# Low parts on VectorE alone, keys split in place, and one factor a row in a single-core hybrid attention layer

## The chip, the cores and the metric

The kernel runs on one core of one Trainium2 chip. A core has five engines with a queue of instructions each: TensorE (PE; PEld are its weight loads), VectorE (DVE), ScalarE (ACT), GpSimd (POOL) and SyncE (SP), which here issues all DMAs. An engine takes its instructions strictly in the order in which they were written; engines wait for each other by semaphores. Matmul results land in PSUM (8 banks of 128x512 float32), everything else that engines work on lies in SBUF. The metric is the device time of one execution in microseconds (us); the kernel before takes 1096.38 us (median of 3 runs, 1095.64 to 1096.85).

## The reference

A decoder layer on x of 512x1024 in float32. All arithmetic is float32, and the output has to be that close to it.

```
h = rmsnorm(x, ln_mix_g);  proj = h @ w_in                 # 1024 x 7728
dq, dk, dv, nq, kc, vc, ksl, vsl, kwn, vwn, ng, mg = split(proj)
y_diff : 8 heads; a = softmax(q0 k0) - lam * softmax(q1 k1); rmsnorm(a @ dv) * subln_g * 0.2
y_nsa  : 16 heads in 4 groups; three attentions on one nq, each times its sigmoid gate:
         compressed blocks (a small MLP on kc, vc), selected blocks (ksl, vsl), window (kwn, vwn)
mixed = sigmoid(mg0) * (y_diff @ w_proj_diff) + sigmoid(mg1) * (y_nsa @ w_proj_nsa)
x = x + mixed @ w_out
x = x + square(relu(rmsnorm(x, ln_mlp_g) @ w_mlp_up)) @ w_mlp_down
```

With 512 tokens every block is selected and the window covers every earlier token, so the selected and the window branch are both plain causal attentions with their own keys and values (branch `b` = 0, 1). All queries and keys pass an rmsnorm per head and a rotation (rope).

## The kernel before

**Split numbers.** To keep float32 accuracy at the fast matmul rate, every factor of a matmul is split into two float32r tiles, a high part (a copy with rounding) and a low part (the factor minus its high part), by `split` (line 462): `copy` may be placed on ACT or DVE, the subtraction on the engines in `lo_engs`. A product is then three matmuls: high-high, high-low, low-high. A weight matrix streams through `WStream` (line 393) in pieces of 128x1024: a DMA into `wraw`, then for each half of 512 columns a high part `whi` and a low part `wlo`; two buffers of each, and a piece is prepared while the one before it is used. `add` in line 1541 registers the pieces of each GEMM and names DVE and POOL as the engines that may make the low parts.

**Streams.** The work is written as Python generators that `Pe.run` (line 72) interleaves by an estimate of TensorE's time: `rope_stream` (norm, rope, transposition and splitting of queries and keys), `side_stream` (compressed blocks), `value_stream` (probabilities transposed, split, and multiplied with values), `score_stream` (scores and softmax), and `filler` (all GEMMs in a fixed order: projections, merge gates, output projections, MLP). GEMM matmuls stand between those of the attention on TensorE's queue.

**Planner.** No instruction is issued where it is written: `Sched.note` (line 205) records it with its dependencies and, for each engine that may run it, a price (`price`, line 167); `flush` (line 272) is a list scheduler that takes the engine that is free first, picks the ready instruction that was written first, and so sets every engine's order and the choice of engine. It models one port that DVE and POOL share: `ported` (line 196) says which instructions hold it, and in lines 323 to 334 an engine whose first choice would find the port taken looks for a ready one that doesn't need it, and otherwise takes the first choice and lets it wait. The instructions themselves carry no trace of this port, it only moves their order.

**Keys.** `k_dups` (line 889) gets four transposed 128x128 blocks in a PSUM bank `ptp`: 64 partitions of one key, 64 of another. It splits the bank into the single buffer `kp`, and four DMAs copy each key's 64 partitions to both halves of its own tile `kk`, as the score matmul wants the key twice, once beside the high and once beside the low part of the query.

**Sparse probabilities.** In `score_stream` (line 1050) each tile of scores `sb` becomes `p` (mask and minimum on DVE, exponential with a row sum on ACT); then DVE makes the reciprocal of the row sum and multiplies `p` with two factors a row, the reciprocal and the gate (lines 1105 to 1107). There are two `p` buffers for each of the three larger widths and four for the smallest.

Names in the rows: `gb`, `ga` GEMM banks; `sb` scores; `sm`, `smn` row statistics of the differential and the sparse heads; `ptn`, `pta` transposed probabilities; `ah`, `al` their parts; `rw`, `t1r`, `t2r`, `str` the rope's; `hT` the normed input; `u`, `rr` the squared ReLU. All instructions are issued from line 357, so tiles tell them apart.

Of the kernel before, what the change touches and what calls it, by code (L numbers as in the profile page):

```python
# [12 lines left out]
F32R = mybir.dt.float32r  # L13
AF = mybir.ActivationFunctionType
# [117 lines left out]
class Sched:  # L132
# [34 lines left out]
    def price(self, eng, method, aps, k):  # L167
        if "accum_out" in k:
            aps = [x for x in aps if x is not k["accum_out"]]
        n = max(self.size(x) for x in aps)  # L170
        psum = any(self.tiles[x.tensor.name].space == "PSUM" for x in aps if x.tensor.name in self.tiles)
        if eng == "PE":
            if method == "transpose":
                return 113.0
            return max(113.0, 5.5 + self.size(aps[-1]) * 0.4315)
        if eng == "ACT":
            return (51 if psum else 93) + n * 0.8333 + (93 if "accum_out" in k else 0) + (
                93 if any(self.size(x) == 1 for x in aps[1:]) and n > 1 else 0)
        if eng == "DVE":
            ptr = sum(1 for x in aps[1:] if self.size(x) == 1) if n > 1 else 0  # L180
            if method in ("tensor_scalar", "tensor_copy") and not psum:
                return 69 + n * 0.52 + 61 * ptr
            if method == "memset":
                return 8 + n * 1.04
            if method == "reciprocal":
                return 69 + n * 6.25
            return 69 + n * 1.042 + 61 * ptr
        if eng == "POOL":
            if k.get("op") == OP.pow:
                return 300 + n * 165.0  # L190
            return 150 + n * 2.1
        return 20.0
# [2 lines left out]

    def ported(self, eng, method, aps, k):

        if max(self.size(x) for x in aps) < 64:
            return False
        if eng == "POOL":  # L200
            return k.get("op") != OP.pow
        return eng == "DVE" and method in self.TWICE and not any(
            self.tiles[x.tensor.name].space == "PSUM" for x in aps if x.tensor.name in self.tiles)

# [67 lines left out]
    def flush(self):  # L272

        ops, self.ops = self.ops, []
        self.wait = {e: [] for e in self.free}
        ok = {e: [] for e in self.free}
        fresh, again = [], set()
        for op in ops:
            for b in op.bufs:
                if b.group is None or b in again:  # L280
                    continue
                again.add(b)
                if b.granted:
                    self.held[b.group] += 1
                else:
                    fresh.append(b)
        for b in fresh:
            self.held.setdefault(b.group, 0)
            self.queue.setdefault(b.group, []).append(b)
        for op in ops:  # L290
            op.left, op.ready = 1, 0.0
            for d in op.deps:
                if d.left == -1:
                    op.ready = max(op.ready, d.end + self.lat(d.eng, op.eng, op.deps[d]))
                else:
                    d.users.append(op)
                    op.left += 1
            for b in op.bufs:
                if not b.granted:
                    b.waiting.append(op)  # L300
                    op.left += 1
        for g in list(self.queue):
            self.grant(g, 0.0)
        for op in ops:
            self.arm(op)
        done = []
        while len(done) < len(ops):
            best = None
            for e in self.free:
                for h, k in ((self.wait[e], 2), (ok[e], 1)):  # L310
                    while h and h[0][k].left == -1:
                        heapq.heappop(h)
                t = self.free[e] if ok[e] else max(self.free[e], self.wait[e][0][0]) if self.wait[e] else None
                if t is not None and (best is None or t < best[0]):
                    best = (t, e)
            assert best is not None, "no instruction can go on"
            t, e = best
            while self.wait[e] and self.wait[e][0][0] <= t:
                _, p, op = heapq.heappop(self.wait[e])
                if op.left == 0:  # L320
                    heapq.heappush(ok[e], (p, op))
            p, op = heapq.heappop(ok[e])
            if op.port[e] and self.port > t:
                put_off = [(p, op)]
                while ok[e] and put_off[-1][1].port[e]:
                    z = heapq.heappop(ok[e])
                    if z[1].left == 0:
                        put_off.append(z)
                if not put_off[-1][1].port[e]:
                    p, op = put_off.pop()  # L330
                else:
                    p, op = put_off.pop(0)
                for z in put_off:
                    heapq.heappush(ok[e], z)
            op.eng = e
            op.start = max(t, self.port) if op.port[e] else t
            op.end = op.start + op.ways[e][1]
            if op.port[e]:
                self.port = op.end
            self.free[e] = op.end  # L340
            if op.dma:
                self.hw = max(op.end, self.hw) + op.dma[0]
                self.dma = max(self.hw + 650, self.dma) + op.dma[1]
                op.end = self.dma
            op.left = -1
            done.append(op)
            for u in op.users:
                u.ready = max(u.ready, op.end + self.lat(e, u.eng, u.deps[op]))
                self.arm(u)
            for b in op.bufs:  # L350
                b.left -= 1
                b.end = max(b.end, op.end)
                if b.left == 0 and b.group is not None:
                    self.held[b.group] -= 1
                    self.grant(b.group, b.end + 150)
        for op in sorted(done, key=lambda o: o.start):
            op.ways[op.eng][0](*op.a, **op.k)  # L357
            op.ways = op.a = op.k = op.users = op.deps = None
# [68 lines left out]
def hybrid_block(ctx: ExitStack, tc: tile.TileContext, x, ln_mix_g, w_in, dqg, dkg, lq1, lk1, lq2, lk2,  # L427
# [22 lines left out]
    def f(ap):  # L450
        return ap.bitcast(F32)
# [3 lines left out]

    def copy(out, src, engs=("ACT", "DVE")):
        sched.note([(e, COPY[e], getattr(sched.engs[e], COPY[e])) for e in engs], (out, src), {})

    def tt(out, a, b, op, engs=("DVE",)):
        sched.note([(e, "tensor_tensor", sched.engs[e].tensor_tensor) for e in engs], (out, a, b), {"op": op})  # L460

    def split(hi, lo, src, hi_engs=("ACT", "DVE"), lo_engs=("DVE",)):

        copy(hi, src, hi_engs)
        tt(lo, src, f(hi), OP.subtract, lo_engs)
# [99 lines left out]
    with ExitStack() as ps:  # L565
# [322 lines left out]

        def k_dups(pt, key):

            kp = att.tile([128, 2, 512], F32R, tag="kp", bufs=1, name="kp")
            split(kp[:, 0, :], kp[:, 1, :], pt)
            if key[0] == "dk":
                kk = k_tile()
                dst = [kk[:, s] for s in range(2)]
            else:

                if key[2] == 0:
                    for s in range(2):
                        group_keys[key[1], s] = k_tile()  # L900
                dst = [group_keys[key[1], s][:, key[2]] for s in range(2)]
            for s in range(2):
                for d in range(2):
                    Q.dma_start(f(dst[s][d * 64:(d + 1) * 64]), f(kp[s * 64:(s + 1) * 64]))
            return dst

        jobs = []
# [142 lines left out]
        def score_stream():  # L1050
# [25 lines left out]
            for p in range(2):  # L1076
# [8 lines left out]
                for h in range(8):  # L1085
                    head = p * 8 + h
                    for b, i in [(b, i) for b in range(2) for i in reversed(range(NT))]:
# [14 lines left out]
                        for b_ in bs:  # L1102
                            st = att.tile([128, 12], F32, tag="sm", bufs=8, name="smn")
                            pr = softmax_num(sb[:, b_ * 128:] if i == 0 else sb, i, st[:, 0:2])
                            V.reciprocal(st[:, 3:4], st[:, 1:2])
                            V.tensor_scalar(pr[:, :n], pr[:, :n], st[:, 3:4],
                                            gates[:, i, head * 3 + 1 + b_:head * 3 + 2 + b_], op0=OP.mult, op1=OP.mult)
                            probs[head, b_, i] = pr
                            there(("pn", head, b_, i)).after(P_LAT + 2.5 * n)
                        s_use(S_LAT + n * len(bs))  # L1110
# [430 lines left out]
        def add(gen, pieces):  # L1541
            for piece in pieces:
                load, width = piece if isinstance(piece, tuple) else (piece, 1024)
                ws.add(load, ("DVE", "POOL"), width)
            plan.append(gen)

        def eight(src):
# [101 lines left out]
```

## Time and profile before

| | us |
|---|---|
| median of 3 runs | 1096.38 |
| the profiled execution | 1096.69 |
| its span, first to last instruction | 1094.9 |
| busy in it: PE, DVE, ACT, POOL | 1053.8, 766.2, 465.6, 477.0 |

The profile is of one execution. Busy time of PE is not work at full rate: its matmuls overlap in the record, and a matmul that waits behind another counts as busy. Whether TensorE runs at full rate is seen in how many matmuls start in a stretch. From about 765 us on the kernel is the MLP; up to about 654 us the attention runs beside the projections; what lies between are the output projections.

### The profile page before, as it was taken

The numbers are of one execution on the slowest core, as the hardware profiler recorded it, in microseconds if no ns is written. First come the engines' busy times: TensorE is split into PE (matmuls) and PEld (weight loads), VectorE is DVE, ScalarE is ACT, GpSimd is POOL, SyncE is SP. The second block draws the span as 40 slices with busy tenths as digits, with TensorE's granted clock in tenths as the row PEclk, the third lists the DMA queues.
The fourth block names the chain that finished last, engine by engine and source line by source line (L and its number), as shares of the span: only waits on it lengthen the run. The fifth ranks groups of instructions, "written<-read, shape, count | busy, mean of one in ns | idle before, by whom it ended". The sixth has DMA issues, their size and how long they took to land.

```text
span 1094.9 us, 15737 instructions
## 1 busy us (share of the span) xinstructions
PE 1053.8 (96%) x5257; PEld 875.6 (80%) x5257; DVE 766.2 (70%) x1905; ACT 465.6 (43%) x1136; POOL 477.0 (44%) x475
## 2 busy tenths in 40 slices
PE   6999988899999999999999998999999999999998
PEld 5877867788787888887788886788888888888886
DVE  6779678899988999999989898556533323354232
ACT  4257335656464466665456563214222111242110
POOL 3745698348767372292212024423333222333221
PEclk9999988999999999999999999999999999999999
DMA  6362534642654224536363255622322223332232
GB/s 209 97 173 63 153 102 120 163 132 71 172 143 142 64 78 137 142 125 214 129 193 112 92 161 170 208 85 94 96 97 97 97 96 96 97 97 96 97 136 75
DMA packets 83616, 134.66 MB, mean 123 GB/s; under 512 B 8784, under 2 KB 33872, under 8 KB 83536
## 3 DMA queue, kind: packets, MB, share of 16 engines
q1 hardware_dynamic: 83536, 133.67, 39.7%
q8 instruction: 41, 0.67, 0.3%
q14 instruction: 39, 0.32, 0.1%
HBM read 106.64 MB, written 14.42 MB: 111 GB/s over the span
## 4 chain that ended last, share of the span: by engine, by line
PE 74%; DVE 12%; DMA 6%; POOL 4%; issue 2%; SPq 1%; ACT 1%; DVEq 0%; POOLq 0%; ACTq 0%
PE gb L357 38%; PE ga L357 22%; PE sb L357 4%; PE avn L357 4%; PE ptn L357 3%; DMA kk<-kp 3%; DVE p L357 2%; POOL str L357 1%; PE av L357 1%; POOL wlo L357 1%; SPq L357 1%; POOL t1r L357 1%; DVE al L357 1%; DVE sm L357 1%; DMA kk<-in_x_dram 1%
## 5 line engine op out<-in xcount | busy, mean ns | idle before, releaser
L357 POOL TENSOR_TENSOR wlo<-wraw,whi 128x512 fp32r<-128x512 f32 x203 | 289.0, 1432 | 522.7 <-ACT whi L357 396.2
L357 ACT CAST whi<-wraw 128x512 fp32r<-128x512 f32 (+2 forms) x217 | 130.0, 618 | 343.7 <-PE gb L357 167.0
L357 DVE CAST whi<-wraw 128x512 fp32r<-128x512 f32 x97 | 47.5, 489 | 199.7 <-PE ga L357 95.8
L357 PE MATMUL gb<-wlo,hTh 128*128 128x512 f32 (+2 forms) x352 | 136.0, 388 | 4.4 <-POOL wlo L357 2.4
L357 PE MATMUL gb<-whi,hTl 128*128 128x512 f32 (+2 forms) x352 | 135.0, 384 | 0.0
L357 PE MATMUL gb<-whi,hTh 128*128 128x512 f32 (+2 forms) x352 | 133.4, 388 | 1.5 <-ACT hTh L357 1.3
L357 DVE CUSTOM_DVE_ANT_0 p<-sb,cst 128x512 f32<-128x512 f32 (+2 forms) x192 | 92.1, 481 | 13.1 <-PE sb L357 11.7
L357 DVE TENSOR_TENSOR wlo<-wraw,whi 128x512 fp32r<-128x512 f32 (+1 forms) x111 | 92.2, 832 | 7.2 <-ACT whi L357 2.7
L357 ACT ACTIVATE p<-p,smn 128x512 f32<-128x512 f32 (+3 forms) x128 | 72.0, 563 | 26.6 <-DVE smn L357 26.2
L357 PEld LDWEIGHTS gb<-wlo,hTh 128*128 128x128 f32 x352 | 67.7, 192 | 14.8 <-POOL wlo L357 3.4
L357 PEld LDWEIGHTS gb<-whi,hTh 128*128 128x128 f32 x352 | 66.7, 191 | 11.5 <-ACT hTh L357 1.7
L357 PEld LDWEIGHTS gb<-whi,hTl 128*128 128x128 f32 x352 | 67.6, 192 | 10.3 <-DVE hTl L357 0.3
L357 DVE TENSOR_SCALAR p<-p,smn,gates 128x512 f32<-128x512 f32 (+3 forms) x128 | 66.9, 527 | 1.0
L357 PE MATMUL gb<-big,whi 128*128 128x512 f32 x192 | 65.1, 403 | 0.0
L357 PE MATMUL gb<-hTl,whi 128*128 128x512 f32 x160 | 64.7, 404 | 0.0
L357 PE MATMUL gb<-hTh,wlo 128*128 128x512 f32 x160 | 64.5, 403 | 0.0
L357 PE MATMUL gb<-hTh,whi 128*128 128x512 f32 x160 | 64.0, 400 | 0.0
L357 DVE TENSOR_TENSOR al<-ptn,ah 128x128 fp32r<-128x128 f32 (+3 forms) x128 | 61.3, 482 | 3.6 <-ACT ah L357 2.0
L357 PE MATMUL ga<-h2l,whi 128*128 128x512 f32 x160 | 62.5, 391 | 0.0
L357 PE MATMUL ga<-h2h,whi 128*128 128x512 f32 x160 | 62.4, 391 | 0.0
L357 PE MATMUL ga<-h2h,wlo 128*128 128x512 f32 x160 | 62.3, 390 | 0.0
L357 ACT CAST ah<-ptn 128x384 fp32r<-128x384 f32 (+3 forms) x98 | 41.2, 424 | 49.1 <-PE ptn L357 38.1
(248 smaller groups left out, 2634.7 us busy)
## 6 DMA issues: line engine op xcount, KB each, us to landing
wraw<-in_w_in_dram SPq DMA_DIRECT2D x36, 512.0 KB, 3.6
wraw<-in_w_mlp_up_dram SPq DMA_DIRECT2D x32, 512.0 KB, 3.8
wraw<-in_w_mlp_down_dram SPq DMA_DIRECT2D x32, 512.0 KB, 3.5
kk<-kp SPq DMA_DIRECT2D x48, 256.0 KB, 4.5
wraw<-in_w_in_dram SPq DMA_DIRECT2D x36, 256.0 KB, 3.2
big<-yd SPq DMA_DIRECT2D x16, 512.0 KB, 3.4
yd<-yo SPq DMA_DIRECT2D x8, 512.0 KB, 3.3
wraw<-in_w_proj_diff_dram SPq DMA_DIRECT2D x8, 512.0 KB, 4.3
```

The costliest lines, as they stand in the source:

```text
L357: op.ways[op.eng][0](*op.a, **op.k)
```

## The change

Four edits, and one in the planner that goes with them. The low parts of weights may only be made by DVE (all but the first chunk, which is registered in another place and keeps both engines). `k_dups` has no `kp` any more: it splits each key's 64 partitions straight into its own half of `kk`, and one DMA a key copies that half to the other. A sparse tile is multiplied with one factor a row: the product of reciprocal and gate is made first, as 128x1 on DVE or POOL, and the product with `p` may go to DVE or ACT. In the planner, an engine whose ready choices all need the taken port now stays open until the port is free or something else becomes ready; DVE instructions of fewer than 64 elements a row count as holding the port too; and a 128x1 `scalar_tensor_tensor` costs one pointer more.

```diff
-            ptr = sum(1 for x in aps[1:] if self.size(x) == 1) if n > 1 else 0
+            ptr = sum(1 for x in aps[1:] if self.size(x) == 1) if n > 1 else method == "scalar_tensor_tensor"
...
     def ported(self, eng, method, aps, k):
-        if max(self.size(x) for x in aps) < 64:
-            return False
         if eng == "POOL":
-            return k.get("op") != OP.pow
+            return k.get("op") != OP.pow and max(self.size(x) for x in aps) >= 64
...
-                if not put_off[-1][1].port[e]:
+                go = not put_off[-1][1].port[e]
+                if go:
                     p, op = put_off.pop()
-                else:
-                    p, op = put_off.pop(0)
                 for z in put_off:
                     heapq.heappush(ok[e], z)
+                if not go:
+                    self.free[e] = min(self.port, self.wait[e][0][0]) if self.wait[e] else self.port
+                    continue
             op.eng = e
-            op.start = max(t, self.port) if op.port[e] else t
+            op.start = t
...
+    def scaled(out, src, factor):
+        sched.note([("DVE", "tensor_scalar", lambda o, x, c: nc.vector.tensor_scalar(o, x, c, None, op0=OP.mult)),
+                    ("ACT", "activation", lambda o, x, c: nc.scalar.activation(o, x, AF.Copy, scale=c))],
+                   (out, src, factor), {})
...
         def k_dups(pt, key):
-            kp = att.tile([128, 2, 512], F32R, tag="kp", bufs=1, name="kp")
-            split(kp[:, 0, :], kp[:, 1, :], pt)
...
             for s in range(2):
-                for d in range(2):
-                    Q.dma_start(f(dst[s][d * 64:(d + 1) * 64]), f(kp[s * 64:(s + 1) * 64]))
+                own, other = slice(s * 64, s * 64 + 64), slice(64 - s * 64, 128 - s * 64)
+                split(dst[s][own, 0], dst[s][own, 1], pt[own])
+                Q.dma_start(f(dst[s][other]), f(dst[s][own]))
...
                             V.reciprocal(st[:, 3:4], st[:, 1:2])
-                            V.tensor_scalar(pr[:, :n], pr[:, :n], st[:, 3:4],
-                                            gates[:, i, head * 3 + 1 + b_:head * 3 + 2 + b_], op0=OP.mult, op1=OP.mult)
+                            tt(st[:, 4:5], st[:, 3:4], gates[:, i, head * 3 + 1 + b_:head * 3 + 2 + b_], OP.mult,
+                               ("DVE", "POOL"))
+                            scaled(pr[:, :n], pr[:, :n], st[:, 4:5])
...
-                ws.add(load, ("DVE", "POOL"), width)
+                ws.add(load, ("DVE",), width)
```

Since the planner sets the order, the edits move instructions on every engine. By count over the whole program: low parts of weights on DVE 111 before and 313 now, on POOL 203 before and 1 now; products with sparse probabilities on DVE 128 before, now 45 there and 83 on ACT; the new 128x1 products 27 on DVE and 101 on POOL; high parts of weights on DVE 97 and 104, on ACT 217 and 210; high parts `ah` of transposed probabilities on DVE 40 and 53, on ACT 120 and 107; copies of projections `rw` out of PSUM on DVE 10 and 13; rope products and sums on DVE 75 and 97, on POOL 125 and 103; subtractions for keys on DVE 12 of 128 partitions before, 24 of 64 now; DMAs of keys 48 before, 24 now. TensorE has the same 5257 matmuls.

DVE, keys of the sixth differential head, before (`qa`, `qb` are the parts of the queries of the same job):

```order
L357 SCALAR_TENSOR_TENSOR p<-p,sm 128x512
L357 CAST kp<-ptp 128x512
L357 ISA p,sm<-sb,cst 128x384
L357 ISA sm 128x1
L357 TENSOR_TENSOR kp<-ptp,kp 128x512
L357 TENSOR_TENSOR qa<-ptp,qa 64x512
L357 TENSOR_TENSOR qb<-ptp,qb 64x512
```

and the same place now:

```order
L357 CAST kk<-ptp 64x512
L357 RECIPROCAL sm<-sm 128x4
L357 ISA p,sm<-sb,cst 128x384
L357 ISA sm 128x1
L357 TENSOR_TENSOR kk<-ptp,kk 64x512
L357 SCALAR_TENSOR_TENSOR sm<-sm,lam 128x1
L357 TENSOR_SCALAR ys<-yt,sm 128x128
L357 CAST kk<-ptp 64x512
L357 TENSOR_TENSOR qa<-ptp,qa 64x512
L357 TENSOR_TENSOR kk<-ptp,kk 64x512
L357 TENSOR_TENSOR qb<-ptp,qb 64x512
```

One split of 128 partitions into `kp` has become two of 64 into `kk`, with other work between them.

POOL, in the differential heads, before (`sm` are the row statistics of a finished head's output):

```order
L357 TENSOR_TENSOR t2r<-rw,ropes 128x4x32
L357 TENSOR_TENSOR t1r<-t1r,t2r 128x512
L357 TENSOR_TENSOR sm<-sm,epsc 128x1
L357 TENSOR_TENSOR sm<-sm,mhalf 128x1
L357 TENSOR_TENSOR wlo<-wraw,whi 128x512 x4
L357 TENSOR_TENSOR sm<-sm,epsc 128x1
L357 TENSOR_TENSOR sm<-sm,mhalf 128x1
L357 TENSOR_TENSOR wlo<-wraw,whi 128x512 x2
```

and now:

```order
L357 TENSOR_TENSOR str<-str,epsc 128x8
L357 TENSOR_TENSOR str<-str,mhalf 128x8
L357 TENSOR_TENSOR t2r<-rw,ropes 128x4x32 x2
L357 TENSOR_TENSOR t1r<-rw,ropec 128x256
L357 TENSOR_TENSOR sm<-sm,epsc 128x1
L357 TENSOR_TENSOR sm<-sm,mhalf 128x1
```

The low parts between the statistics and the rope's steps are gone from POOL's queue.

DVE, in the sparse heads, before:

```order
L357 RECIPROCAL smn<-smn 128x1
L357 ISA p,smn<-sb,cst 128x384
L357 ISA smn 128x1
L357 TENSOR_TENSOR pc<-sc,st_1557 128x256
L357 TENSOR_SCALAR p<-p,smn,gates 128x512
L357 ISA p,smn<-sb,cst 128x256
L357 ISA smn 128x1
L357 RECIPROCAL smn<-smn 128x1
L357 TENSOR_SCALAR p<-p,smn,gates 128x384
L357 CAST ah<-ptn 128x128
```

and now, a little later in the same stage:

```order
L357 RECIPROCAL smn<-smn 128x1
L357 TENSOR_TENSOR al<-ptn,ah 128x256
L357 CAST whi<-wraw 128x512
L461 TENSOR_SCALAR p<-p,smn 128x512
L357 TENSOR_TENSOR al<-ptn,ah 128x384
L357 RECIPROCAL smn<-smn 128x1
L357 ISA p,smn<-sb,cst 128x256
L357 ISA smn 128x1
L357 TENSOR_TENSOR wlo<-wraw,whi 128x512
L357 TENSOR_TENSOR al<-ptn,ah 128x512
L357 CAST ah<-ptn 128x128
L357 TENSOR_TENSOR wlo<-wraw,whi 128x512
```

One of the two products with `p` has left DVE's queue, and two low parts of weights stand in it.

## Rows read from the trace of the kernel before

**Rows 1.** Page, parts 1 and 2: busy time by engine, TensorE's clock by slice

```profile
PE 1053.8 (96%) x5257; PEld 875.6 (80%) x5257; DVE 766.2 (70%) x1905; ACT 465.6 (43%) x1136; POOL 477.0 (44%) x475
...
PEclk9999988999999999999999999999999999999999
```

**Rows 2.** Page, part 4: the chain that ended last, by engine, by line

```profile
PE 74%; DVE 12%; DMA 6%; POOL 4%; issue 2%; SPq 1%; ACT 1%; DVEq 0%; POOLq 0%; ACTq 0%
PE gb L357 38%; PE ga L357 22%; PE sb L357 4%; PE avn L357 4%; PE ptn L357 3%; DMA kk<-kp 3%; DVE p L357 2%; POOL str L357 1%; PE av L357 1%; POOL wlo L357 1%; SPq L357 1%; POOL t1r L357 1%; DVE al L357 1%; DVE sm L357 1%; DMA kk<-in_x_dram 1%
```

**Rows 3.** The chain from 765 us: start, length, what, count

```profile
873.43 43.52 PE ga L357 x192
```

**Rows 4.** Stretches: width; PE, PEld, DVE, ACT, POOL busy (instructions); PEclk, DMA share, GB/s

```profile
0.00:150.00 150.00, 138.47 (x687) 114.59 (x688) 113.58 (x271) 71.34 (x168) 86.75 (x97) 1.00 0.44 130
150.00:210.00 60.00, 50.13 (x249) 40.65 (x247) 49.20 (x120) 31.49 (x78) 39.30 (x46) 0.86 0.57 149
210.00:654.00 444.00, 432.91 (x2412) 364.64 (x2411) 411.82 (x1204) 262.43 (x713) 208.32 (x242) 1.00 0.43 131
...
765.00:1095.00 330.00, 326.02 (x1438) 269.57 (x1436) 119.04 (x197) 66.32 (x111) 103.01 (x67) 1.00 0.30 98
```

**Rows 5.** Timeline of PE: start, us, operation, [idle before it, and who ended it]

```profile
157.46 0.70 PE L357 MATMUL ptp<-cst,rw 128*128 128x128 f32 x4 [2.76 <-DVE kp L357]
...
175.65 0.80 PE L357 MATMUL gb<-wlo,hTh 128*128 128x512 f32 x1 [1.82 <-DVE wlo L357]
...
199.84 0.50 PE L357 MATMUL sb<-kk,qa 128*128 128x256 f32 x2 [2.40 <-DVE sm L357]
```

**Rows 6.** Timeline of DVE at three places

```profile
16.84 2.47 DVE L357 TENSOR_TENSOR hTl<-ga,hTh 128x512 fp32r<-128x512 f32 x4
...
173.77 1.22 DVE L357 SCALAR_TENSOR_TENSOR sm<-sm,lam 128x1 f32<-128x1 f32 x1
...
198.62 0.69 DVE L357 CAST kp<-ptp 128x512 fp32r<-128x512 f32 x1 [2.84 <-DMA kk<-kp]
```

**Rows 7.** Stretch of half clock, columns as in rows 4

```profile
175.00:180.00 5.00, 4.35 (x15) 3.75 (x16) 5.00 (x13) 1.29 (x3) 5.00 (x4) 0.50 0.36 105
```

**Rows 8.** Waits of PE, 0 to 660 us: total us, times, longest

```profile
PE sb L357 <- DVE sm L357: 7.5, 10, 2.4
...
PE gb L357 <- POOL wlo L357: 2.4, 2, 1.7
PE gb L357 <- DVE wlo L357: 2.0, 2, 1.8
```

**Rows 9.** Tile wlo in stretches: PE, PEld, DVE, POOL busy (instructions), then as rows 4

```profile
0.00:150.00 150.00, 69.32 (x188) 35.91 (x189) 20.74 (x22) 36.48 (x27) 1.00 0.44 130
150.00:210.00 60.00, 19.45 (x54) 11.25 (x54) 2.31 (x3) 15.73 (x12) 0.86 0.57 149
210.00:654.00 444.00, 159.06 (x416) 78.80 (x417) 18.13 (x21) 101.62 (x78) 1.00 0.43 131
```

**Rows 10.** Groups by form: busy us, mean ns of one, idle before

```profile
L357 DVE TENSOR_TENSOR wlo<-wraw,whi 128x512 fp32r<-128x512 f32 x110 | 91.7, 834 | 7.2 <-ACT whi L357 2.7 <-issue 0.4
L357 DVE TENSOR_TENSOR al<-ptn,ah 128x512 fp32r<-128x512 f32 x32 | 21.8, 681 | 1.3 <-ACT ah L357 0.6 <-PE ptn L357 0.6
L357 POOL TENSOR_TENSOR wlo<-wraw,whi 128x512 fp32r<-128x512 f32 x201 | 287.6, 1439 | 522.7 <-ACT whi L357 396.2 <-DVE whi L357 51.2 <-PE ga L357 19.3
L357 POOL TENSOR_TENSOR sm<-sm,epsc 128x1 f32<-128x1 f32 x32 | 11.8, 368 | 29.5 <-ACT ysq L357 29.5
```

**Rows 11.** Page, parts 5 and 6: groups, and DMA issues (KB each, us to landing)

```profile
L357 ACT ACTIVATE p<-p,smn 128x512 f32<-128x512 f32 (+3 forms) x128 | 72.0, 563 | 26.6 <-DVE smn L357 26.2
L357 DVE TENSOR_SCALAR p<-p,smn,gates 128x512 f32<-128x512 f32 (+3 forms) x128 | 66.9, 527 | 1.0
...
kk<-kp SPq DMA_DIRECT2D x48, 256.0 KB, 4.5
```

**Rows 12.** Tile kp: who ended the idle time before its instructions (us, times)

```profile
  DMA kk<-kp: 11.4, 6
```

## The prediction

> **What bounds the kernel now.** I read the page's busy times and TensorE's clock first, then the chain, then stretches, and last the single waits. The reader is to see that TensorE looks busy for 96% of the span [rows 1], but that only 74% of the chain is TensorE's; VectorE holds 12% of it, DMAs 6%, GpSimd 4% [rows 2]. The last third settles itself: there 192 matmuls of 512 columns take 43.52 us, 0.227 us each, and the chain is nothing but TensorE [rows 3], at a clock of 1.00 [rows 4]. From 765 us on there is nothing to gain. So the question is about 0 to 654 us, where the attention runs beside the projections. There VectorE is busy for 113.6 + 49.2 + 411.8 = 574.6 us, 88%, and in 210 to 654 us for 411.8 of 444, 92.8% [rows 4]; GpSimd is busy for 334.4 us. TensorE and VectorE feed each other through few buffers, and both are nearly full.
>
> The worst stretch is 150 to 210 us. TensorE's granted clock is 0.86 there on average [rows 4], and 0.50, its lower level of 1.2 GHz, in 175 to 180 us [rows 7]; at 0.86, 60 x 0.14 = 8.4 us of full-rate work are lost. What TensorE did before: it stood still for 2.76 us until VectorE had split keys, for 1.82 us until a low part of a weight came, and for 2.40 us until a row statistic freed a score bank [rows 5]. The first and the third go back to the buffer `kp`: in front of the third VectorE stands for 2.84 us at a key's copy, whose buffer a DMA is still reading [rows 6]. The second low part came late because the operation ahead of it, of one element a row, took 1.22 us, twice what a 128x512 operation costs [rows 6].
>
> **Low parts.** GpSimd makes 27 + 12 + 78 = 117 of them before 654 us [rows 9], and these go to VectorE. A recorded 128x512 operation takes 0.68 us on VectorE when one input is in PSUM; a row of four takes 2.47 [rows 6], so each further one costs (2.47 - 0.68) / 3 = 0.60, and the last 0.08 of a record overlaps with the next. 117 x 0.60 = +70.2 us of VectorE. On GpSimd they took 1.44 us each [rows 10], so a piece's low half is made in less than half the time once its turn comes.
>
> What comes back is the time in which the two engines hold each other up. A low part on VectorE, both inputs in SBUF, takes 0.834 us on average, the operation of the same shape with an input in PSUM 0.681 [rows 10]: 0.153 us, or 18%, is lost beside GpSimd. The share of GpSimd's busy time that goes away is 153.8 of 334.4, 46% [rows 4, 9]. If nothing comes back, 0; if all of VectorE's 574.6 us suffered like the low parts, 0.18 x 0.46 x 574.6 = 48. I take 30, nearer the upper end, since the low parts are the long ones of GpSimd's instructions. The Trainium skill ("SBUF — State Buffer", section "Who interferes with whom") says that a VectorE instruction with two SBUF inputs and a GpSimd instruction that reads SBUF shut each other out, whichever starts first, for the whole instruction. By that rule the trace agrees for the low parts (0.834 against 0.681), and each that is left on GpSimd could cost up to its own 1.44; worked out from it, as an estimate, the relief would lie above my 30.
>
> **Keys.** Twelve splits of 128 partitions become 24 of 64. The time goes by the 512 columns, so VectorE gets 12 more subtractions, +7.2 us; the extra copies go to ScalarE, which is busy for 262.4 of 444 us [rows 4]. Half of the 48 DMAs of 4.5 us each [rows 11] go, all in SP's queue, which only gets shorter. What goes from the path is the wait for `kp`: it ended 11.4 us of idle time [rows 12], of which TensorE saw 2.76 and 2.40 [rows 5]: -5.2. Late next is the key's own tile: the split now writes where the score matmuls of an earlier head read, but these stand earlier in TensorE's queue.
>
> **Sparse probabilities.** 83 of 128 products leave VectorE. One takes 0.527 recorded [rows 11], 0.447 without the overlap: -37.1 us. ScalarE gets 83 operations like the exponential, at most 0.563 each [rows 11], 46.7 us; it has 181 free in 210 to 654. 27 small products on VectorE cost 2 us at most. 101 go to GpSimd at 0.368, the row of its 128x1 addition [rows 10]: 37 us, less than the 101.6 that its low parts leave there. So a link is added: reciprocal, GpSimd, then ScalarE, behind whose product casts of weights and probabilities queue. If GpSimd is late, TensorE waits for these casts; the free time on GpSimd is the cover, and without it the price is bounded by 83 x 0.368 = 31 us of ScalarE, inside its 181. I take 0.
>
> **Planner.** The port rule and the load move a further 22 rope instructions, 13 high parts and 3 copies to VectorE, at most 0.60 each, 23 us; many are shorter, I take 15.
>
> **The sum.** VectorE up to 654 us: 574.6 + 70.2 + 7.2 + 15 + 2 - 37.1 - 30 = 601.9, 92% instead of 88%. What that costs I read in 210 to 654, where it is fullest: 411.8 + 78 x 0.60 + 3.6 (half of the keys) + 10 (of the 15) - 37.1 = 435.1, less two thirds of the relief, 20, is 415.1. If VectorE can again be kept busy for 92.8%, the stretch takes 447.3 us instead of 444: +3.3, I take +4 with the part before 210, where VectorE stays under 90%. Gains: keys -5.2; the two low-part waits of TensorE, 2.4 and 2.0 [rows 8], -4.4; the half clock of 150 to 210 us, -8.4, because the waits ahead of it go. Together -18 + 4 = -14. The MLP gives nothing and takes nothing: its 67 low parts on GpSimd [rows 4] cost VectorE 40 us on top of 119 of 330, and a piece lasts 24 x 0.227 = 5.4 us against 1.2 for its two low parts. If they got stuck behind the squared ReLU, a us at each of eight blocks would be 8 us. So the span goes from 1094.9 to 1080.9; the execution takes 1.8 us more than its span, and it was 0.3 above the median: 1082.5 us.
>
> **Rivals.** A, slower: VectorE becomes the bound in 210 to 654 us. For it speak the 92.8%, and that 70 us of work come onto the engine that most of TensorE's waits already name [rows 8]; against it, that ScalarE takes 37 off. Without any relief 435.1 / 0.928 = 468.9 us, +24.9, less 5.2 for the keys: 1116; with some, anything from 1098 up, 1107 in the middle. It decides where the relief in this stretch is under about 6 us, since (435.1 - 6) / 0.928 - 444 = 18 eats all gains. The Trainium skill's "Perfetto Trace Analysis", section "Optimizing Scalar/DVE Operations", speaks for A: where VectorE is saturated, it advises handing work to ScalarE or even GpSimd, the opposite of what is done with the low parts; it adds that between VectorE and GpSimd this might not help, because of their common port. Which half of it holds is what the trace of before leaves open.
>
> B, faster by much more: the chain's pieces that the change shortens all vanish, DMA kk<-kp 3%, POOL wlo, str and t1r 1% each [rows 2], 6% or 66 us. Against it: another chain takes over. Half of it, 33 us, gives 1063.
>
> C, no change: TensorE is busy for 96% [rows 1], its named waits are small [rows 8], and a new order makes new ones of the same size, each with a fall of the clock. 1096.
>
> **Chances.** Forecast 0.50, between 1076 and 1090; B 0.15; C 0.10; A 0.25. Half of B lies under 1066 and half of A above 1107, which leaves a fifth outside. A difference under 0.2% can't be told from none: faster 0.65, same 0.10, slower 0.25.
>
> **What would show it.** Right: in the profile after, no wait of TensorE for a key's copy between 150 and 210 us, and PEclk there near 1.00; low parts on VectorE near 0.70 us instead of 0.834; VectorE's busy time up by about 70 us over the whole span (27 before 654, 40 after); the last score product some 14 us before 654; matmuls from 765 us on at 0.227. Wrong: TensorE's waits for VectorE's low parts and row statistics well above the 9.5 us of before, VectorE above 95% from 210 us on, or half clock at new places; then A holds. If the last third is slower than 0.227 a matmul, low parts got stuck in the MLP, which I cost at nothing.

## The result, and the profile after

| | before | changed |
|---|---|---|
| median of the runs, us | 1096.49 | 1078.11 (1077.22 to 1079.62) |
| ratio, 95% interval | | 0.9827 [0.9814, 0.9840] |
| profiled execution; its span, us | 1096.69; 1094.9 | 1078.69; 1076.8 |

The change is faster by 18 to 19 us. The prediction was 1082.5, range 1066 to 1107. First, busy times, clock and chain of the changed kernel, as in [rows 1, 2]:

```profile
PE 1047.9 (97%) x5257; PEld 871.5 (81%) x5257; DVE 801.1 (74%) x2110; ACT 500.2 (46%) x1210; POOL 190.5 (18%) x348
...
PEclk9999999999999999999999999999999999999999
...
PE 77%; DVE 13%; DMA 4%; POOL 2%; issue 2%; ACT 1%; SPq 0%; DVEq 0%; ACTq 0%
PE gb L357 40%; PE ga L357 21%; PE sb L357 5%; PE avn L357 4%; PE ptn L357 3%; DVE wlo L357 2%; DVE p L357 1%; PE av L357 1%; DVE kk L357 1%; PE hb L357 1%; POOL str L357 1%; DVE qa L357 1%; PE pta L357 1%; DVE qb L357 1%; DVE t1r L357 1%
```

GpSimd went from 477 to 190 us, VectorE up by 35. In the chain the copies of keys (DMA, 3%) have shrunk to a single one of 4.92 us, and DMA and GpSimd together fell from 10% to 6%. Next the stretches, columns as in [rows 4]:

```profile
0.00:150.00 150.00, 139.40 (x690) 114.75 (x691) 122.23 (x317) 72.41 (x172) 46.63 (x63) 1.00 0.42 127
150.00:210.00 60.00, 52.96 (x287) 43.69 (x285) 55.85 (x153) 35.78 (x94) 24.82 (x37) 0.94 0.43 117
210.00:654.00 444.00, 439.03 (x2438) 369.70 (x2437) 413.72 (x1273) 294.13 (x773) 117.78 (x247) 1.00 0.41 127
654.00:765.00 111.00, 108.57 (x491) 88.71 (x490) 70.30 (x130) 32.94 (x63) 1.29 (x1) 1.00 0.43 139
```

Read the counts of matmuls behind PE's busy time: against [rows 4], 3 more are recorded up to 150 us, 38 more in 150 to 210, 26 more in 210 to 654. The clock of the second stretch rose from 0.86 to 0.94. The chain's piece that answers to [rows 3]:

```profile
855.32 43.52 PE ga L357 x192
```

It starts at 855.32 instead of 873.43 us, 18.11 earlier, which is the whole difference of the spans (18.1); the 192 matmuls still take 43.52. TensorE's waits, 0 to 660 us, as in [rows 8]:

```profile
PE sb L357 <- DVE sm L357: 3.1, 6, 0.7
PE pta L357 <- DVE kk L357: 2.0, 1, 2.0
...
PE gb L357 <- DVE wlo L357: 1.5, 2, 1.0
```

The wait for row statistics fell from 7.5 to 3.1 us, that for low parts from 4.4 to 1.5, that for `kp` has gone, and one for a key's split, at 193.6 us, is new. Behind it the clock falls once more, columns as in [rows 4]:

```profile
195.00:200.00 5.00, 4.41 (x24) 4.38 (x25) 4.25 (x15) 1.85 (x6) 0.00 (x0) 0.66 0.22 43
```

The low parts on VectorE, by form, as in [rows 10]:

```profile
L357 DVE TENSOR_TENSOR wlo<-wraw,whi 128x512 fp32r<-128x512 f32 x310 | 207.1, 691 | 5.0 <-PE gb L357 0.5 <-ACT whi L357 0.4
```

0.691 us instead of 0.834, and so about that of the operation of the same shape with an input in PSUM.

### The profile page after: what moved, and what is told of

Read it like the earlier page. It is cut to its first block, busy times and chain, and to the rows that moved or that the text cites. A ratio compares the mean times of both kernels' runs of the same rounds, so it can differ in the third digit from the quotient of the medians.

```text
span 1076.8 us, 15772 instructions
## 1 busy us (share of the span) xinstructions
PE 1047.9 (97%) x5257; PEld 871.5 (81%) x5257; DVE 801.1 (74%) x2110; ACT 500.2 (46%) x1210; POOL 190.5 (18%) x348
## 4 chain that ended last, share of the span: by engine, by line
PE 77%; DVE 13%; DMA 4%; POOL 2%; issue 2%; ACT 1%; SPq 0%; DVEq 0%; ACTq 0%
PE gb L357 40%; PE ga L357 21%; PE sb L357 5%; PE avn L357 4%; PE ptn L357 3%; DVE wlo L357 2%; DVE p L357 1%; PE av L357 1%; DVE kk L357 1%; PE hb L357 1%; POOL str L357 1%; DVE qa L357 1%; PE pta L357 1%; DVE qb L357 1%; DVE t1r L357 1%
## 5 line engine op out<-in xcount | busy, mean ns | idle before, releaser
L357 ACT CAST whi<-wraw 128x512 fp32r<-128x512 f32 x210 | 126.0, 618 | 328.7 <-PE gb L357 180.6
L357 DVE TENSOR_TENSOR wlo<-wraw,whi 128x512 fp32r<-128x512 f32 x313 | 208.4, 689 | 5.0 <-PE gb L357 0.5
L357 DVE CAST whi<-wraw 128x512 fp32r<-128x512 f32 x104 | 44.2, 427 | 184.6 <-PE ga L357 91.8
L357 PEld LDWEIGHTS gb<-wlo,hTh 128*128 128x128 f32 x352 | 66.9, 190 | 11.9 <-DVE wlo L357 2.4
L357 POOL TENSOR_TENSOR smn<-smn,gates 128x1 f32<-128x1 f32 x101 | 23.9, 240 | 241.6 <-DVE smn L357 241.6
L357 PE MATMUL ga<-whi,u 128*128 128x512 f32 x192 | 59.7, 389 | 0.0
L357 PE MATMUL gb<-whi,u 128*128 128x512 f32 x192 | 59.6, 389 | 0.0
```

## The experiments

All of them use the change's own hunks or add a few lines. Differences in us below are (ratio to before - 1) x 1096.4, since the runs of one kernel on several chips differ by a us or two. The diffs show the lines of an edit that tell it from the others, not the whole of it.

### One edit alone, on the kernel before

`a_low` has only the last hunk of the diff, `a_keys` only that of `k_dups`, `a_scale` only `scaled` and its call, `a_plan` only those of the planner. `n_before` changes nothing but a number of the planner, and with it the order:

```diff
# a_low
-                ws.add(load, ("DVE", "POOL"), width)
+                ws.add(load, ("DVE",), width)
# a_keys
+                split(dst[s][own, 0], dst[s][own, 1], pt[own])
+                Q.dma_start(f(dst[s][other]), f(dst[s][own]))
# a_scale
+                            scaled(pr[:, :n], pr[:, :n], st[:, 4:5])
# a_plan
+                if not go:
+                    self.free[e] = min(self.port, self.wait[e][0][0]) if self.wait[e] else self.port
+                    continue
# n_before
-SLACK = 250
+SLACK = 255
```

Expected of a_low:

> The kernel before, with low parts of weights on VectorE alone and nothing else of the change. Theory (the prediction's sum): without the 37 us that the sparse products give back, VectorE has 411.8 + 78 x 0.60 - 20 = 438.6 us to do in the stretch that lasted 444 us, so that at a fill of 92.8% it lasts 473 us, and the kernel takes about 1115 us. Rival: what VectorE gets back from GpSimd is larger than 20 us in this stretch, as after shows 413.7 us there where the sum had 415.1 with more work on it; then the low parts alone give a good part of the 18 us, and the time is near 1090.

Of a_keys:

> The kernel before, with only the keys split into their own half, without the key buffer. Theory: TensorE's waits of 2.76 and 2.40 us go and with them two falls of the clock, some 3 us each: 1085 to 1089. Rival: a new order of instructions puts other waits in their place, 1096 plus or minus 4.

Of a_scale:

> The kernel before, with only one factor a row for the sparse probabilities, on VectorE or ScalarE. Theory: VectorE loses 37 us of work in a stretch in which it is full to 92.8%; if it sets the pace there, 1070 to 1080; if TensorE does, 1090 or more. I expect 1088. Rival: the added link through GpSimd, behind its low parts of 1.44 us, comes late, and the time is 1096 or above.

Of a_plan:

> The kernel before, with only the planner's edit: an engine whose choices all need the port stays open, small VectorE instructions count as holding the port, and one price. Theory: the order changes and the work doesn't, 1096 plus or minus 4. Rival: the planner's edit is what removes the falls of the clock, 1080 to 1088.

Of n_before:

> The kernel before with the same allowance of 255 ns instead of 250: the same work in a slightly other order. If a slight change of order is worth as much as the single edits on the kernel before (-5, -5, +3.4, +11 us), this one is off by 3 us or more; if not, 1096 plus or minus 2.

| kernel | us | ratio, interval | difference, us | VectorE busy in 210 to 654 us | GpSimd, DMA in the chain |
|---|---|---|---|---|---|
| a_low | 1092.14 | 0.9964 [0.9953, 0.9975] | -3.9 | 420.3 | 6%, 6% |
| a_keys | 1092.15 | 0.9960 [0.9948, 0.9972] | -4.4 | 407.8 | 4%, 4% |
| a_scale | 1100.46 | 1.0038 [1.0023, 1.0052] | +4.2 | 405.5 | 4%, 6% |
| a_plan | 1108.04 | 1.0102 [1.0082, 1.0122] | +11.2 | 404.9 | 6%, 7% |
| n_before | 1096.12 | 0.9997 [0.9986, 1.0008] | -0.3 | 407.8 | 6%, 6% |

All four lie outside the range of my theory. The keys come nearest: they did about what the prediction priced (-5.2), and no more than that, as the falls of the clock that were to go with their waits came in other places (0.94 instead of 0.86 in 150 to 210 us, but 0.99 instead of 1.00 in 210 to 654; over the span 0.992, before 0.990). The sum of the prediction falls with `a_low`: VectorE has more to do in its fullest stretch, 420.3 of 444 us, and the kernel is faster. `a_scale` is the reverse, less work there and slower. In it TensorE waits longer for the sparse row statistics (1.1 us in 3 waits before):

```profile
PE sb L357 <- DVE smn L357: 4.0, 7, 1.0
```

In `a_plan` the wait for the key buffer grew, which was 11.4 us [rows 12]. First, from the view of tile `kp`, what its instructions' engines stood idle for; then TensorE's waits:

```profile
  DMA kk<-kp: 20.2, 5
```

```profile
PE ptc L357 <- DVE kp L357: 3.9, 1, 3.9
...
PE sb L357 <- DMA kk<-kp: 2.4, 2, 1.3
```

So the planner's edit makes an order that leans harder on the key buffer. That this is all of its 11 us is not shown. The four single differences add up to +7 us and all four edits together give -19: 26 us lie in what they do for each other. Three of the four must be read with care: `n_before`, a mere change of order, is one draw and moved the time by 0.3 us, but the same change of the changed kernel moves it by 4.3 (`n_after`, below), as much as each of -3.9, -4.4 and +4.2. That these three come from the edits themselves is not shown.

### One edit taken back, from the changed kernel

Each kernel is the changed one with one of the four hunks undone, and `n_after` is the changed one with `SLACK = 255`.

```diff
# u_low
-                ws.add(load, ("DVE",), width)
+                ws.add(load, ("DVE", "POOL"), width)
# u_keys
+            split(kp[:, 0, :], kp[:, 1, :], pt)
+                    Q.dma_start(f(dst[s][d * 64:(d + 1) * 64]), f(kp[s * 64:(s + 1) * 64]))
# u_scale
-                            scaled(pr[:, :n], pr[:, :n], st[:, 4:5])
# u_plan
+                else:
+                    p, op = put_off.pop(0)
-                if not go:
```

Expected of u_low:

> The changed kernel, with the low parts of weights on VectorE or GpSimd again, the rest of the change kept. Singly the edits gave -5 (low parts), -5 (keys), +3.4 (factors) and +11 us (planner); their sum, +4.4, is far from the -18 of all four, so at least two of them pay only together. Theory: it is the low parts on GpSimd that make the factors' product and the planner's edit dear (a 128x1 product waits behind low parts of 1.44 us; an engine that stays open for the port leaves low parts undone), so with them back on GpSimd the time is 1095 to 1110. Rival: the keys are the partner that the other edits need; then low parts are worth their single 5 us here too, about 1083.

Of u_keys:

> The changed kernel, with the key buffer and its four DMAs a bank again. Theory: the keys are worth here what they are worth alone, 5 us: 1083. Rival: they are the partner that the other edits need, with 1090 or more.

Of u_scale:

> The changed kernel, with the sparse product of two factors on VectorE again. Theory: VectorE gets 37 us back in a stretch in which it is full, so 1090 to 1100. Rival: the factors cost by themselves (a_scale, +3.4 us), and without them the time is 1075 to 1079.

Of u_plan:

> The changed kernel, with the planner of before. Theory: without low parts on GpSimd the port is seldom contended and the planner's edit does little, 1078 plus or minus 4. Rival: the edit costs here what it costs alone, 11 us, and without it the time is near 1067.

Of n_after:

> The changed kernel with the planner's allowance for a link between engines at 255 ns instead of 250: the same work, with some hundred of TensorE's instructions in other places. A yardstick: if the new order as such moves the time, this one does too, by 5 us or more; if what the edits do sets it, 1078 plus or minus 2.

| kernel | us | ratio, interval | lost against the changed kernel, us | VectorE busy in 210 to 654 us | GpSimd, DMA in the chain | mean clock |
|---|---|---|---|---|---|---|
| changed | 1078.11 | 0.9827 [0.9814, 0.9840] | | 413.7 | 2%, 4% | 0.997 |
| u_low | 1078.48 | 0.9839 [0.9824, 0.9854] | 1.3 | 398.9 | 3%, 4% | 0.998 |
| u_keys | 1092.99 | 0.9962 [0.9945, 0.9978] | 14.8 | 404.7 | 3%, 6% | 0.991 |
| u_scale | 1084.78 | 0.9896 [0.9882, 0.9910] | 7.6 | 423.9 | 2%, 4% | 0.995 |
| u_plan | 1089.83 | 0.9936 [0.9921, 0.9951] | 12.0 | 404.7 | 6%, 4% | 0.998 |
| n_after | 1080.97 | 0.9866 [0.9849, 0.9882] | 4.3 | 411.9 | 2%, 3% | 0.994 |

The losses are differences of the ratios; by the two intervals each is uncertain by about 2 us. `n_after` is the yardstick, though a single draw: an order that is merely another one costs 4 us here. The keys and the planner's edit stand well above it, the factors a little, the low parts not at all. Of my theories none held: `u_keys` went as its rival said, `u_scale` lies between theory and rival, and `u_plan` went against both, which had the edit do little or cost 11 us.

**u_low** refutes my theory and its rival together. Low parts may go to GpSimd again and the time is the same. The changed planner sends fewer there and lets fewer of them meet, and it does so in `a_plan` as well, where it is the only edit. By form, first in `u_low`, then in `a_plan`:

```profile
L357 DVE TENSOR_TENSOR wlo<-wraw,whi 128x512 fp32r<-128x512 f32 x206 | 142.7, 721 | 5.6 <-ACT whi L357 1.0
L357 POOL TENSOR_TENSOR wlo<-wraw,whi 128x512 fp32r<-128x512 f32 x105 | 140.2, 1345 | 478.0 <-DVE whi L357 363.2 <-ACT whi L357 88.7 <-PE ptn L357 6.8
```

```profile
L357 DVE TENSOR_TENSOR wlo<-wraw,whi 128x512 fp32r<-128x512 f32 x209 | 146.1, 726 | 6.1 <-ACT whi L357 1.4
L357 POOL TENSOR_TENSOR wlo<-wraw,whi 128x512 fp32r<-128x512 f32 x102 | 137.4, 1357 | 609.6 <-DVE whi L357 396.6 <-ACT whi L357 161.2 <-PE gb L357 33.5
```

105 and 102 instead of 201 on GpSimd, and those on VectorE take 0.721 and 0.726 us, not 0.834 [rows 10]. That the low parts cost nothing in `u_low` for this reason fits these numbers, but is not shown. VectorE is also emptier, which buys nothing: up to 654 us, in the changed kernel and in `u_low` (columns as in [rows 4]):

```profile
0.00:654.00 654.00, 631.38 (x3410) 528.14 (x3411) 591.79 (x1741) 402.32 (x1038) 189.23 (x347) 0.99 0.42 126
```

```profile
0.00:654.00 654.00, 630.00 (x3417) 528.14 (x3417) 574.20 (x1702) 398.73 (x1026) 282.01 (x402) 1.00 0.42 126
```

17.6 us less of VectorE, as many matmuls done.

**u_keys** brings the key buffer back, and with it 15 us: the tile's view names it, and the page's chain holds the DMA again:

```profile
  DMA kk<-kp: 15.7, 6
```

```profile
PE 74%; DVE 12%; DMA 6%; POOL 3%; ACT 2%; issue 2%; SPq 1%; DVEq 0%; ACTq 0%; POOLq 0%
PE gb L357 39%; PE ga L357 21%; PE sb L357 4%; PE avn L357 3%; DMA kk<-kp 3%; PE ptn L357 3%; POOL str L357 2%; DVE wlo L357 1%; PE av L357 1%; PE hb L357 1%; SPq L357 1%; DVE p L357 1%; DVE t1r L357 1%; DVE t2r L357 1%; POOL t1r L357 1%
```

Every kernel here that has `kp` shows DMA at 6 or 7% of the chain, every one without it 3 to 5%. About 6.5 us of the 14.8 are clock: 1077 x (0.997 - 0.991). The rest is not: the one execution of `u_keys` that ran at a clock of 1.000 took 1086.79 us, still 8.7 above the changed kernel.

**u_plan** has no clock to blame (0.998). The order of before gives GpSimd more of the rope (132 of its products and sums instead of 103; its busy time is 229.8 instead of 190.5 us), and VectorE stands for it. What ended VectorE's idle time ahead of the rope's last product, from the view of the tile `str` that it reads, in `u_plan` and in the changed kernel:

```profile
  POOL t1r L357: 11.9, 7
```

```profile
  POOL t1r L357: 1.7, 1
```

The chain's share of GpSimd is 6% instead of 2%. By itself that share decides nothing: `n_before` has 6% too, at the time of before. That the rope's wait is the whole of the 12 us is not shown.

### GpSimd's load put back, with every order kept

Two kernels make GpSimd busy again beside two of three of VectorE's low parts, in the order of the changed kernel on all other engines; the extra results are not used. `shadow` reads as much from SBUF as a low part on GpSimd does, `shadow_p` almost nothing. Both read the weights in `wraw`, so that this buffer comes free only behind the extra work.

```diff
+        r = nc.vector.tensor_tensor(o, a, b, op=op)
# shadow
+            nc.gpsimd.tensor_tensor(junk[:, :w], a[:, c:c + w], a[:, c:c + w], op=OP.add)
# shadow_p
+        nc.gpsimd.tensor_tensor(junk[:, :8], epsc[:, :8], a[:, :8], op=OP.pow)
```

Expected of shadow:

> The changed kernel with every engine's order kept, and on GpSimd, beside 204 of VectorE's low parts, four additions of 128x128 with weights from SBUF, whose results nothing uses: GpSimd's load of before without its work. Theory (the prediction's relief): GpSimd's load holds VectorE up, so the low parts on VectorE go from 0.69 back to 0.83 us, VectorE's busy time up to 654 us rises by 20 to 40 us, and if its fill sets the pace (the step that charged +4 for a fuller VectorE), the time is 1095 to 1105. Rival: VectorE is held up but doesn't set the pace, as u_low, with 15 us less work on VectorE from 210 to 654 us and the same time, suggests; then the time is 1079 to 1088. Second rival: nothing is held up, low parts stay at 0.69 us.

Of shadow_p:

> As the kernel named shadow, with every engine's order kept, but the work that GpSimd has beside 204 of VectorE's low parts is one power of 128x8, some 1.88 us by the row of its power on row statistics, instead of four additions of 128x128, 2.03 us: nearly the same time in GpSimd's queue, with 1/64 of the numbers read. Its results are not used either. Theory, after shadow took 1150 us and its chain went through GpSimd for 18% (2% in the changed kernel): it is the queue on GpSimd, behind which the rope's steps, the row statistics and the sparse factors stand, so the time is again 1130 to 1155, with VectorE's low parts back at 0.69 to 0.70 us. Rival: it is the access to SBUF that GpSimd and VectorE share, which showed as 0.75 us a low part and 45 us more of VectorE's time; then this one takes 1078 to 1090.

Measured: `shadow` 1149.99 us, 1.0476 [1.0456, 1.0497]; `shadow_p` 1110.40 us, 1.0132 [1.0115, 1.0149]. Against the changed kernel that is +71 and +33 us. `shadow` lies above all its forecasts, and its low parts took 0.754 us, not 0.83; `shadow_p` lies between its two. By form, the extra work and the low parts, first of `shadow`:

```profile
L474 POOL TENSOR_TENSOR junk<-wraw 128x128 f32<-128x128 f32 x814 | 413.9, 509 | 272.8 <-DMA wraw<-in_w_mlp_up_dram 84.7 <-DMA wraw<-in_w_mlp_down_dram 73.8 <-DMA wraw<-in_w_in_dram 29.9
L471 DVE TENSOR_TENSOR wlo<-wraw,whi 128x512 fp32r<-128x512 f32 x202 | 147.6, 754 | 6.1 <-ACT whi L357 3.1 <-PE gb L357 0.3
```

and of `shadow_p`:

```profile
L472 POOL TENSOR_TENSOR junk<-epsc,wraw 128x8 f32<-128x8 f32 x204 | 357.4, 1752 | 276.1 <-DMA wraw<-in_w_mlp_up_dram 107.5 <-DMA wraw<-in_w_mlp_down_dram 96.6 <-DMA wraw<-in_w_in_dram 30.2
L471 DVE TENSOR_TENSOR wlo<-wraw,whi 128x512 fp32r<-128x512 f32 x202 | 134.1, 688 | 3.8 <-ACT whi L357 0.7 <-PE gb L357 0.3
```

In `shadow_p` nothing holds VectorE up (0.688 us a low part, 804.6 us busy against 801.1), so its 33 us come of what waits for GpSimd, whose share of the chain is 13%:

```profile
PE 68%; POOL 13%; DVE 11%; DMA 4%; issue 3%; ACT 1%; SPq 0%; DVEq 0%; POOLq 0%; ACTq 0%
```

The rope's steps stand behind the extra work in its queue. And the DMAs of the next weights stand behind it too, as it holds `wraw`, and ScalarE's copies behind these; in the changed kernel the first of these two waits is not there, and the second is 0.7 us:

```profile
SPq L357 <- POOL junk L472: 60.8, 37, 4.8
```

```profile
ACT whi L357 <- DMA wraw<-in_w_in_dram: 12.1, 6, 5.9
```

How the 33 us divide between the two is not shown.

In `shadow` VectorE is busy for 846.7 us, 45 more, and the time is 38 us above that of `shadow_p`; its extra work is 16% longer (413.9 against 357.4 us), which by the same measure is some 5 of them, and its clock is lower (0.983 against 0.991), some 9 more. So GpSimd's load costs twice where the order was not made for it: some 33 us by what waits for it, and, what is left of the 38, up to some 24 by what it holds up on VectorE. My theory and its rival were both half right. `u_low` shows the other side: where the planner knows the load, 105 low parts on GpSimd cost nothing.

None of the kernels run is faster than the changed one.

## Why the prediction was right in its number and not in its terms

**Right.** The last third: 43.52 us for 192 matmuls, nothing gained or lost. Low parts at 0.69 us, forecast 0.70. TensorE's waits went the forecast way: low parts -2.9 of -4.4, `kp` -5.2, less the new 2.0 us at 193.6 us for a key's split, where none was expected. Two of the signs that were to show it right did not come: the clock of 150 to 210 us is 0.94, not near 1.00, and VectorE's busy time is up by 35 us, not 70.

**The relief** was the step that was most in doubt, taken at 30 with bounds of 0 and 48. Summed over VectorE's forms up to 654 us (the smaller count of the two kernels times the fall of the mean, for example 32 x (0.533 - 0.340) = 6.2 for `ys`), it is 55 us, over the upper bound: not only low parts were held up, short operations were too. For that reason VectorE was busy for 591.8 us there, not 601.9, although more was done in that time, and over the whole span for 35 us more than before, not 70. But the low parts are not the only cause. Summed in the same way, `a_low`, where they alone left GpSimd, has 51; `u_low`, with 83 of the 117 still there in this stretch, has 44; and `a_plan`, the planner's edit alone, has 43. Either edit gives most of it.

**A fuller VectorE, +4.** Wrong. The step read 92.8% as the fill that sets the pace; five kernels show that it doesn't: 398.9, 404.9, 413.7, 420.3 and 423.9 us of the same 444 go with 1078, 1108, 1078, 1092 and 1085 us. The two edits that stand well above the yardstick work on links instead, the key's buffer and DMA (`u_keys`) and the rope's steps on GpSimd (`u_plan`). The Trainium skill's "Perfetto Trace Analysis", section "Optimizing Scalar/DVE Operations", spoke for rival A with its advice to hand work away from a saturated VectorE; of its two halves the runs bear out the other one, that between VectorE and GpSimd this might not help: with 105 low parts on GpSimd or with one the time is the same (1.3 us, uncertain by 2).

**Keys, -5.2.** As a single edit -4.4, as forecast. In company 14.8, some 6.5 of them clock: mis-sized, because I counted only TensorE's two waits for `kp`, and not the 3% of the chain [rows 2] and the 11.4 us of VectorE's and ScalarE's idle time [rows 12] that the same buffer held. Rival B had read that row, and the result lies between the two.

**Planner, priced as 15 us more of VectorE's work and no gain.** Missed: 12 us in company. The rope instructions that it moves to VectorE (22 by the prediction's count, 29 against `u_plan`) were taken for a load alone; in company their move goes with a shorter wait for `t1r` (11.9 us in `u_plan`, 1.7 with the edit). Alone, in `a_plan`, the edit moves 33 of them and costs 11 us, so why it pays only beside the others stays open.

**Factors.** The 37 us of VectorE's time were about right for the products, but VectorE's whole busy time is only 14 us lower than without the edit (801.1 against 815.3 in `u_scale`), since the planner gives VectorE other work instead, 9 more of the rope's instructions and 5 more high parts of weights; the 27 small products cost 4.8 us, where 2 was the bound. 7.6 us of time follow, 3 above the yardstick. The added link, taken at 0, does no harm in company, though ScalarE waits 17.9 us for it; alone the edit costs 4.2 us, and there ScalarE waits less for it (13.4 us), so its waits do not show low parts in front of the product as the cause.

**The clock, -8.4.** (0.94 - 0.86) x 60 = 4.8 us came in 150 to 210; another (1.00 - 0.98) x 111 = 2.2 us came in 654 to 765, where before TensorE had stood 3.3 us for `big`; not forecast. The stretch and the wait of before:

```profile
654.00:765.00 111.00, 106.29 (x479) 86.21 (x479) 72.53 (x117) 34.01 (x67) 39.58 (x26) 0.98 0.43 143
```

```profile
PE ga L357 <- DVE big L357: 3.3, 1, 3.3
```

The 3.6 us of the term that did not come lie in falls at new places, the one to 0.66 behind the key's split among them.

So the sum met the measured time because keys and planner gave more than their terms while the low parts, for whose sake VectorE's account was drawn up, gave nothing in company. That these errors cancel to 4 us is luck. What stays open: which of the planner's three rules does it, and whether keys and planner alone would give the 18 us; those kernels were not run.

## What to carry to other kernels

Where two engines feed each other through few buffers, read the chain and the idle time that a single buffer or link ends, also on the engine that isn't the bottleneck, before adding up busy time: a fill of 90 or 95% of VectorE told nothing here. An instruction that is moved changes three things, the engine's load, the queue behind it and what it holds up elsewhere, and a scheduler that knows them can make the move itself worthless. Price each edit alone and taken back, with mere changes of order as the yardstick, more than one of them (one said 0.3 us here, the other 4.3): single edits of -4, -4, +4 and +11 us gave -19 together.

## What the runs showed of the hardware

A GpSimd instruction of 1.68 us need not hold up VectorE at all. `shadow_p`, GpSimd and then VectorE at the same time:

```profile
310.93 1.68 POOL L472 TENSOR_TENSOR junk<-epsc,wraw 128x8 f32<-128x8 f32 x1
```

```profile
311.03 0.69 DVE L471 TENSOR_TENSOR wlo<-wraw,whi 128x512 fp32r<-128x512 f32 x1
...
311.78 0.68 DVE L471 TENSOR_TENSOR wlo<-wraw,whi 128x512 fp32r<-128x512 f32 x1
```

Two low parts run inside one power of 128x8 at their undisturbed length. The Trainium skill ("SBUF — State Buffer", sections "SBUF: two separate sides" and "Who interferes with whom") has the two shut each other out for the whole instruction when GpSimd reads SBUF; for additions of 128x128 the trace goes in its direction (0.754 us a low part on average), for the power of 128x8, which reads SBUF too, it does not (0.688 us over 202 low parts, 0.691 in the changed kernel).

Short VectorE operations lose as well beside a loaded GpSimd: the 128x1 `SCALAR_TENSOR_TENSOR` on `sm`, 32 of them, took 0.322 us before and 0.239 after, and 0.255 in `a_low`, where only the low parts had left GpSimd.
